# The opening of a diffusion-block kernel: x turned by channel tile, scale and shift by rows, P5 by halves of K in front of P2

## The chip, the cores and the metric

The kernel runs on one core of one Trainium2 chip. The metric is the device time of one execution in microseconds (us), lower is better. Engines: TensorE (PE, matrix products), VectorE (DVE), ScalarE (ACT), GpSimd (POOL) and SyncE (SP), whose queue issues the DMAs. Each works through a list of its own in order; semaphores make one wait for another.

## The reference

One layer of a hybrid diffusion backbone over x (1024 tokens x 1024 channels), all in float32. What the opening of the kernel computes is this part, with `sh1` and `sc1` from a small product of SiLU(c) with `w_mod`:

```
sh1, sc1, gt1, sh2, sc2, gt2 = adaln(c, w_mod, b_mod)
h = rmsnorm(x, g_pre1) * (1 + sc1) + sh1
q, k, v, f, g_a, g_f = split_proj(h @ w_in)
```

Attention over windows, a Fourier branch, the merge of both and a gated convolutional feed-forward net follow. They are not touched by the change.

## The kernel before

**The large products.** `h @ w_in` and `h2 @ w_up` are made by Strassen-Winograd: a pair of 128-wide output columns and two halves of the 1024 tokens give seven products P1 to P7 instead of eight, each over half of K (four tiles of 128 channels). The moving operands come from h: B11, B21, B22 are quarters of it (turned, channels on the partitions, 512 tokens wide), and T1, T2, T3, T4n are their differences. T1 is the token difference of the first four channel tiles; T2 and T4n are taken from T1's raw tile; T3 from the other half. P1 reads B11, P2 B21, P3 B22, P4 T4n, P5 T1, P6 T2, P7 T3. The stationary operands A11 to A22 and their sums S1 to S4 come from the weights. Each product is made of float32 parts: an operand is split into a high part (`hi`, a cast on ACT, L80) and a low part (`lo`, a subtraction on DVE, L68), and three matmuls hi\*hi, hi\*lo, lo\*hi are summed (L85 to L87). An item of four channel tiles is thus 12 matmuls of 128x512.

**The opening** is written out by hand (`with tc.manual_schedule()`): the order of calls is the order of each engine's list. It covers the first 17 items, which are P1, P2, P5, P6 and P7 of the first three pairs (pairs g0, g1, g2), then P4 and P3 of the first. From item 17 on a loop sets the order. The stages:

- Loads. SP issues x (eight tiles of 128 tokens, two halves each), four stages of `w_mod` for shift and scale (`ws`, 256 columns of each a stage, `wm_stage`), the A quarters, the rope tables, and six groups of `w_mod` for the later gates (`wa`, `wm`, `ada_load`). SP keeps eight issues under way and waits for the oldest.
- x. Squares on ACT (`x_square`), root and a Newton step (`x_norm`, two token tiles at a time), scaling by the norm (`x_scale`), turning on PE (`transpose8`, `x_turn`, L162 and L996).
- Shift and scale. `mod_rows` (L581) makes rows of the product with SiLU(c), `mod_copy` (L585) brings them out of PSUM, `mod_turn` (L592) makes columns of them, `mod_vec` adds biases and gains to `ax` and `sx`, two channel tiles a stage, for the latents (c=0) and the context (c=1).
- h. Scale and shift by `affine` (L547 on ACT, L549 on DVE): since a turned token tile has four channel tiles side by side, an instruction covers 128x128. `hraw` holds h by token tile; `hb_puts` and `hb_part` write the operands with one cast and one subtraction per token tile, 384 and 128 wide (or 128 or 256 wide in parts).
- `ada_rows`, `ada_copy` (L749, L753): the gate groups, rows of the product with later columns of `w_mod`.

**Places.** PSUM has eight banks (`ps`, `bufs=8`). The stages `ws`, the gate groups `wa` and the operands other than B11 and T1 share the places of one pool (tag `ha`, ten); a tile that takes over a place is written when the readers of the last one are done.

Of the kernel before, what the change touches and what calls it, by code (L numbers as in the profile page):

```python
# [13 lines left out]
ALU = mybir.AluOpType  # L14
# [26 lines left out]
def block_kernel(ctx: ExitStack, tc: tile.TileContext, t: dict, out: bass.AP, dbg: dict):  # L41
# [497 lines left out]
        else:  # L539
            eng.tensor_scalar(out=xs[tk][h], in0=xs[tk][h], scalar1=xr_[tk], scalar2=1.0, op0=ALU.mult, op1=ALU.mult)  # L540

    def affine(out, src, kh, eng, ks):
        for k in ks:
            a, b = ax[:, 0, kh * 4 + k:kh * 4 + k + 1], sx[:, 0, kh * 4 + k:kh * 4 + k + 1]
            o, i = out[:, k * P:(k + 1) * P], src[:, k * P:(k + 1) * P]
            if eng is None:
                nc.scalar.activation(out=o, in_=i, func=AF.Identity, scale=a, bias=b)  # L547
            else:
                eng.tensor_scalar(out=o, in0=i, scalar1=a, scalar2=b, op0=ALU.mult, op1=ALU.add)  # L549

    def x_turn(tk):
        pt[tk] = transpose8(xs[tk], ps, f"x{tk}")

    pt = {}

    def x_raw(tk):

        hraw[tk, 1] = s(f"hr{tk}1")
        copy(hraw[tk, 1], pt[tk][1])

    def x_first(tk, ks=range(4), kh=0, eng=None):
        if ks[0] == 0:
            hraw[tk, kh] = s(f"hr{tk}{kh}")
        affine(hraw[tk, kh], pt[tk][kh], kh, eng, ks)

    def x_second(tk, ks, eng):
        affine(hraw[tk, 1], hraw[tk, 1], 1, eng, ks)


    modp = {}  # L570
# [24 lines left out]
    def mod_vec(q):  # L595
        k0, ks = 2 * q, slice(2 * q, 2 * q + 2)
        for c in range(2):
            add(sx[:, c, ks], modp[q][:, c:4:2], vec[:, VSH1 + k0:VSH1 + k0 + 2])
            add(ax[:, c, ks], modp[q][:, 4 + c:8:2], vec[:, VSC1 + k0:VSC1 + k0 + 2])
            nc.vector.scalar_tensor_tensor(out=ax[:, c, ks], in0=ax[:, c, ks], scalar=1.0, in1=vec[:, VG1 + k0:VG1 + k0 + 2],  # L600
                                           op0=ALU.add, op1=ALU.mult)


    w_in = t["w_in"]
# [296 lines left out]
    at(NI - 14, lambda: late_loads(0))  # L901
    run, lead, main, pre, conv, sums, mm, evac, after, st = wino(pairs, items, ps, hooks, seng=[nc.vector])
    with tc.manual_schedule():
        for tk in range(4):
            x_load(tk)
        wm_stage(0)
        wm_stage(1)
        for j in range(3):
            pre(j, ("A11",))
        wm_stage(2)  # L910
        wm_stage(3)
        x_load(4)
# [17 lines left out]
        for tk in range(2):  # L930
            for i in range(2):
                x_scale(tk, i, nc.vector)
        x_turn(0)
        x_turn(1)
        x_norm(2)
        mod_rows(0, range(4))
        for tk in range(2, 4):
            for i in range(2):
                x_scale(tk, i, nc.vector)
        x_raw(0)  # L940
        x_raw(1)
        x_turn(2)
        x_turn(3)
        x_raw(2)
        x_raw(3)
        mod_rows(0, range(4, 8))
        mod_copy(0)
        mod_turn(0)
        mod_vec(0)
        def alt_(i):  # L950
            return nc.vector if i % 2 else None

        for c in range(4):
            x_first(c, (0, 1), 0, alt_(c))
        hb_part(hb, "B11", {c: hraw[c, 0] for c in (0, 2, 1, 3)}, 0, 2)
        mod_rows(1, range(8))
        ada_load(0, range(KT))
        conv(0, "P1")
        mm(0, range(2))
        mod_copy(1)  # L960
        conv(1, "P1")
        mod_turn(1)
        mod_vec(1)
        for tk in range(4):
            x_first(tk, (2, 3), 0, alt_(tk))
        mm(1, range(2))
        conv(2, "P1")
        hb_part(hb, "B11", {c: hraw[c, 0] for c in (0, 2, 1, 3)}, 2, 4)
        mm(2, range(2))
        mod_rows(2, range(8))  # L970
        ada_load(1, range(KT))
        mm(0, range(2, 4))
        mod_copy(2)
        mod_turn(2)
        mm(1, range(2, 4))
        mod_vec(2)
        engs = (nc.vector, None, None, nc.vector)
        b21 = {c: hraw[c, 1] for c in (0, 1, 3, 2)}
        for c in range(4):
            x_second(c, (0, 1), engs[c])  # L980
        mod_rows(3, range(4))
        mm(2, range(2, 4))
        mod_rows(3, range(4, 8))
        ada_load(2, range(KT))
        hb_part(hb, "B21", b21, 0, 2)
        conv(0, "P2")
        mod_copy(3)
        mod_turn(3)
        x_square(4)
        x_square(5)  # L990
        mod_vec(3)

        def turn(tk, kh):
            p_ = ps(f"ptx{tk}{kh}")
            for k in range(4):
                nc.tensor.transpose(p_[:, k * P:(k + 1) * P], xs[tk][kh][:, k * P:(k + 1) * P], ident)  # L996
            pt.setdefault(tk, {})[kh] = p_

        def t1(c, eng=None):
            sub(hraw[c, 0], hraw[c + 4, 0], hraw[c, 0], eng)  # L1000

        for c in range(4):
            x_second(c, (2, 3), engs[c])
        hb_part(hb, "B21", b21, 2, 4)
        mm(3)
        x_norm(4)
        for tk in (4, 5):
            x_scale(tk, 0, nc.vector)
        conv(1, "P2")
        x_square(6)  # L1010
        x_square(7)
        for tk in (4, 5):
            turn(tk, 0)
        conv(2, "P2")
        mm(4)
        x_norm(6)
        for tk in (6, 7):
            x_scale(tk, 0, nc.vector)
        for tk in (4, 5):
            x_first(tk, range(4), 0, alt_(tk))  # L1020
        ada_rows(0, 0)
        for tk in (6, 7):
            turn(tk, 0)
        for tk in (6, 7):
            x_first(tk, range(4), 0, alt_(tk))
        mm(5)
        ada_rows(0, 1)
        for c in range(4):
            t1(c)
        sums(0, "S1")  # L1030
        hb_puts(hb, "T1", {c: hraw[c, 0] for c in range(4)})
        conv(0, "P5")
        ada_copy(0)
        ada_load(3, range(KT))
        for tk in range(4, 8):
            x_scale(tk, 1, None)
        ada_rows(1, 0)
        ada_rows(1, 1)
        ada_copy(1)
        ada_load(4, range(KT))  # L1040
        for tk in (4, 5):
            turn(tk, 1)
        for j in range(3):
            evac(j)
        for j in range(3, 6):
            evac(j, True)
        sums(1, "S1")
        conv(1, "P5")
        for tk in (4, 5):
            x_first(tk, range(4), 1)  # L1050
        mm(6)
        for tk in (6, 7):
            turn(tk, 1)
        sums(2, "S1")
        conv(2, "P5")
        for tk in (6, 7):
            x_first(tk, range(4), 1)
        mm(7)
        ada_rows(2, 0)
        for j in range(3):  # L1060
            sums(j, "S3")
            sums(j, "S2")
        conv(0, "P6")
        mm(8)
        ada_rows(2, 1)
        for c in range(4):
            sub(hraw[c, 0], hraw[c + 4, 1], hraw[c, 0])
        hb_puts(hb, "T2", {c: hraw[c, 0] for c in range(4)})
        ada_copy(2)
        ada_load(5, range(KT))  # L1070
        ada_rows(3, 0)
        ada_rows(3, 1)
        conv(1, "P6")
        conv(2, "P6")
        ada_copy(3)
        mm(9)
        ada_rows(4, 0)
        for j in range(4, 9):
            after(j)
        evac(9)  # L1080
        for c in range(4):
            sub(hraw[c + 4, 0], hraw[c + 4, 1], hraw[c + 4, 0])
        mm(10)
        ada_rows(4, 1)
        hb_puts(hb, "T3", {c: hraw[c + 4, 0] for c in range(4)})
        mm(11)
        ada_rows(5, 0)
        for j in range(3):
            conv(j, "P7")
        ada_copy(4)  # L1090
        evac(10)
        evac(11)
        for c in range(4):
            sub(hraw[c, 0], hraw[c, 1], hraw[c, 0])
        for k in range(-12, 12):
            lead(k)
        mm(12)
        ada_rows(5, 1)
        hb_puts(hb, "T4n", {c: hraw[c, 0] for c in range(4)})
        mm(13)  # L1100
        mm(14)
        hb_puts(hb, "B22", {c: hraw[c + 4, 1] for c in range(4)})
        ada_copy(5)
        for k in range(12, 15):
# [1118 lines left out]
```

## Time and profile before

| | us |
|---|---|
| time, median of 3 (1324.95 to 1325.07) | 1325.01 |
| profiled execution, its own time | 1326.39 |
| its span | 1324.6 |
| PE busy | 1266.2 (96%) |
| DVE busy | 1046.2 (79%) |
| ACT busy | 691.2 (52%) |
| first large product starts at | 26.9 |
| first product with T4n starts at | 108.1 |

The page's second part shows the span in 40 slices of 33 us. PE is busy 5 tenths of the first slice and 8 of the next two; from the fourth on it is at 9 almost throughout. DMA is at 9 in the first two. The opening covers the first three slices and a little more. A row of the timeline reads: start, length, engine, line, operation, written tile <- read tiles, shape, number of merged instructions, and in brackets how long the engine was idle before and who ended that. Clock is the share of full speed granted to PE.

### The profile page before, as it was taken

What the parts mean: (1) busy time and instruction counts of PE and PEld (TensorE: products, weight loads), DVE (VectorE), ACT (ScalarE), POOL (GpSimd) and SP (SyncE); (2) the same over time, 40 slices, a digit from 0 to 9 for tenths busy, and PEclk for the clock granted to TensorE, in tenths of its full rate; (3) what the DMA queues carried; (4) which work ended last, traced back from release to release, by engine and by line L of the source; (5) the groups of instructions that cost most, each with busy time, mean ns of one, the idle gap of its engine ahead of it and who ended that gap; (6) DMA issues with size and microseconds to landing.
All of it is one profiled execution on the core that took longest, in us unless ns stands there. A gap on an engine that the chain in (4) does not pass through costs nothing.

```text
span 1324.6 us, 18599 instructions
## 1 busy us (share of the span) xinstructions
PE 1266.2 (96%) x5976; PEld 1021.8 (77%) x5976; DVE 1046.2 (79%) x1954; ACT 691.2 (52%) x1418; POOL 231.3 (17%) x191
## 2 busy tenths in 40 slices
PE   5889999999999999899999999999999999999996
PEld 3457877888878877678877888888888887888884
DVE  4687685976698997676879998999888878666767
ACT  5685245633567775344476655454445445544442
POOL 0000120200243334000000033445545200000000
PEclk9999999999999999999999999999999999999999
DMA  9986275432524443855312487777866668987883
GB/s 307 365 287 204 97 254 175 130 89 85 141 72 121 120 133 99 273 172 162 110 40 67 124 253 233 222 207 222 251 203 198 198 200 292 372 267 223 288 289 144
DMA packets 271575, 254.57 MB, mean 192 GB/s; under 512 B 16733, under 2 KB 206837, under 8 KB 271477
## 3 DMA queue, kind: packets, MB, share of 16 engines
q1 hardware_dynamic: 271476, 253.38, 61.2%
q8 instruction: 47, 0.77, 0.2%
q14 instruction: 52, 0.42, 0.1%
HBM read 179.65 MB, written 73.40 MB: 191 GB/s over the span
## 4 chain that ended last, share of the span: by engine, by line
PE 68%; DVE 15%; DMA 8%; ACT 4%; issue 3%; SPq 2%; POOL 1%; DVEq 0%; ACTq 0%; POOLq 0%
PE X_u L87 5%; PE X_u L85 5%; PE X_u L86 5%; PE X_d L87 3%; PE X_d L85 3%; PE X_d L86 3%; PE Y_u L85 3%; PE Y_u L87 3%; PE Y_u L86 3%; DVE p L1289 2%; PE X_g L85 2%; PE X_g L86 2%; PE X_g L87 2%; DMA ws<-in_w_mod 2%; DVE pl L68 2%
## 5 line engine op out<-in xcount | busy, mean ns | idle before, releaser
L68 DVE TENSOR_TENSOR lP_u<-A_u,hP_u 128x512 fp32r<-128x512 f32 x132 | 106.8, 813 | 22.9 <-ACT hP_u L307 21.3
L369 ACT COPY snP_u<-X_u 128x512 f32<-128x512 f32 x57 | 33.5, 587 | 131.7 <-PE X_u L87 131.6
L369 ACT COPY snP_d<-X_d 128x512 f32<-128x512 f32 x48 | 28.2, 588 | 98.0 <-PE X_d L87 93.8
L307 ACT CAST hP_u<-A_u 128x512 fp32r<-128x512 f32 x121 | 74.7, 620 | 0.0
L1309 POOL TENSOR_SCALAR p<-p,sm 128x640 f32<-128x640 f32 (+1 forms) x64 | 48.5, 780 | 91.7 <-PE pp L1314 35.3
L80 ACT CAST ph<-pp 128x512 fp32r<-128x512 f32 x76 | 44.3, 585 | 22.5 <-PE pp L1314 21.3
L68 DVE TENSOR_TENSOR pl<-pp,ph 128x512 fp32r<-128x512 f32 x76 | 51.6, 681 | 2.5 <-ACT ph L80 2.1
L68 DVE TENSOR_TENSOR yd<-yd,snP_d 128x512 f32<-128x512 f32 x36 | 24.9, 691 | 34.2 <-ACT snP_d L369 34.0
L1303 ACT ACTIVATE p<-p,nm 128x640 f32<-128x640 f32 (+1 forms) x64 | 51.3, 802 | 0.7 <-DVE nm L1296 0.7
L68 POOL TENSOR_TENSOR A_u<-A_u,A_u 128x512 f32<-128x512 f32 x28 | 47.9, 1711 | 13.9 <-DVE lP_u L68 6.1
L1289 DVE CUSTOM_DVE_ANT_0 p<-ss,mask 128x640 f32<-128x640 f32 (+1 forms) x64 | 49.9, 781 | 0.0
L1314 PE MATMUL pp<-ident,p 128*128 128x128 f32 x304 | 46.6, 273 | 2.8 <-POOL p L1309 1.5
L1314 PEld LDWEIGHTS pp<-ident,p 128*128 128x128 f32 x304 | 37.2, 140 | 11.7 <-POOL p L1309 2.9
L1724 DVE SCALAR_TENSOR_TENSOR tb<-u,vec,tb 128x1024 f32<-128x1024 f32 x22 | 39.5, 1797 | 3.1 <-ACT tb L1721 3.1
L68 DVE TENSOR_TENSOR lP_g<-A_g,hP_g 128x512 fp32r<-128x512 f32 x48 | 33.4, 700 | 7.7 <-ACT hP_g L80 7.7
L68 POOL TENSOR_TENSOR S_u<-A_u,A_u 128x512 f32<-128x512 f32 x14 | 23.7, 1696 | 88.3 <-DMA g_d0P<-ghP 81.8
L1285 PE MATMUL ss<-kst,qs 128*128 128x384 f32 (+1 forms) x128 | 36.6, 368 | 1.3 <-DVE mx L1289 0.8
L1725 DVE SCALAR_TENSOR_TENSOR tb<-u,vec,tb 128x1024 f32<-128x1024 f32 x22 | 36.5, 1658 | 0.9
L68 POOL TENSOR_TENSOR A_u<-S_u,A_u 128x512 f32<-128x512 f32 x14 | 18.7, 1338 | 104.1 <-DVE lP_u L68 101.7
L68 DVE TENSOR_TENSOR wB<-wB,wB 128x512 f32<-128x512 f32 x44 | 36.0, 817 | 0.0
L1325 PE MATMUL po<-pl,vst 128*128 128x512 f32 x76 | 31.3, 411 | 2.8 <-DVE pl L68 2.3
L1728 ACT ACTIVATE tb<-tb 128x1024 f32<-128x1024 f32 x22 | 23.4, 1063 | 16.6 <-DVE tb L1725 16.6
(887 smaller groups left out, 4378.7 us busy)
## 6 DMA issues: line engine op xcount, KB each, us to landing
A_u<-in_w_up SPq DMA_DIRECT2D x88, 256.0 KB, 4.6
wB<-in_w_down SPq DMA_DIRECT2D x44, 256.0 KB, 4.4
wa<-in_w_mod SPq DMA_DIRECT2D x36, 256.0 KB, 5.3
wt_dT<-wB SPq DMA_DIRECT2D x33, 256.0 KB, 2.3
wdB<-in_w_down SPq DMA_DIRECT2D x33, 256.0 KB, 4.4
wdT<-wt_dT SPq DMA_DIRECT2D x33, 256.0 KB, 3.2
A_g<-in_w_in SPq DMA_DIRECT2D x32, 256.0 KB, 5.5
ws<-in_w_mod SPq DMA_DIRECT2D x30, 256.0 KB, 6.0
```

The costliest lines, as they stand in the source:

```text
L68: return (eng or nc.vector).tensor_tensor(out=out, in0=a, in1=b, op=op)
L80: copy(hi, src)
L85: nc.tensor.matmul(ps, ah, bh, start=start, stop=False, skip_group_check=True)
L86: nc.tensor.matmul(ps, ah, bl, start=False, stop=False, skip_group_check=True)
L87: nc.tensor.matmul(ps, al, bh, start=False, stop=stop, skip_group_check=True)
L307: copy(st[j]["half", p][0], st[j][STA[p]])
L369: copy(d["s" + p], d["X"])
L1289: nc.vector.tensor_tensor_reduce(out=p_, in0=ssc[:, lo:768], in1=self.mk, op0=ALU.add, op1=ALU.max, scale=1.0, scalar=-3.0e38, accum_out=s ...
L1303: nc.scalar.activation(out=self.pt[g], in_=self.pt[g], func=AF.Exp, scale=SCALE, bias=self.m[:, g:g + 1], accum_out=self.sm[:, g:g + 1])
L1309: nc.gpsimd.tensor_scalar(out=self.pt[g], in0=self.pt[g], scalar1=self.sm[:, g:g + 1], scalar2=1.0, op0=ALU.mult, op1=ALU.mult)
L1314: nc.tensor.transpose(pp[:, g * P:(g + 1) * P], self.pt[g][:, j * P:(j + 1) * P], ident)
L1724: nc.vector.scalar_tensor_tensor(out=tb, in0=u[:, 0:1024], scalar=cw[0], in1=tb, op0=ALU.mult, op1=ALU.add)
```

## The change

Nothing is computed otherwise. In the opening:

- Turning goes by channel tile: `x_turn(half, k)` puts one channel tile of four token tiles into one bank, so that scale and shift are one column pair for a whole 128x512 bank. `x_mod` does them in one instruction; `x_raw`, `x_first`, `x_second` and `affine` go. `hraw` is kept by channel tile, and `x_put` splits one of them into its part of an operand: one cast and one subtraction of 128x512.
- `mod_vec` is called for latents and context apart, the latents first.
- Token tiles 4 to 7 of x are requested ahead of the third `w_mod` stage; the A quarters are spread among the stages; the rope tables come behind three gate groups.
- P5 of the first two pairs is made by halves of K ahead of P2; P5 of the third comes behind P2.
- T1, T2, T3 and T4n are made a channel tile at a time: subtraction, cast, low part.
- The gate groups are read later, each whole, behind P5 and between the items of P6, P7 and P4.
- `warm(n)` turns the identity into a bank that nothing reads, 6, 8 and 8 times, at three places where PE waits.

On DVE, the operand T3 (`hr` is `hraw`). Before:

```order
L68 TENSOR_TENSOR hr_695<-hr_842,hr_695 128x512
L68 TENSOR_TENSOR hr_700<-hr_847,hr_700 128x512
L68 TENSOR_TENSOR hr_720<-hr_881,hr_720 128x512
L68 TENSOR_TENSOR hr_725<-hr_886,hr_725 128x512
L68 TENSOR_TENSOR T3a_249<-hr_695,T3a_248 128x3x128
L68 TENSOR_TENSOR T3a_249<-hr_700,T3a_248 128x3x128
L68 TENSOR_TENSOR T3a_249<-hr_720,T3a_248 128x3x128
L68 TENSOR_TENSOR T3a_249<-hr_725,T3a_248 128x3x128
```

and now:

```order
L68 TENSOR_TENSOR hr_556<-hr_735,hr_556 128x512
L68 TENSOR_TENSOR T3a_245<-hr_556,T3a_244 128x512
L68 TENSOR_TENSOR hr_558<-hr_737,hr_558 128x512
L68 TENSOR_TENSOR T3a_245<-hr_558,T3a_244 128x512
L68 TENSOR_TENSOR hr_596<-hr_774,hr_596 128x512
L68 TENSOR_TENSOR T3a_245<-hr_596,T3a_244 128x512
L68 TENSOR_TENSOR hr_598<-hr_776,hr_598 128x512
L68 TENSOR_TENSOR T3b_247<-hr_598,T3b_246 128x512
```

Four subtractions stood ahead of the low parts; now each low part, which reads what its cast on ACT wrote (T3a_244), stands between two subtractions.

On ACT, the casts of T4n and what stands around them, with the semaphores that each waits for. Before:

```order
L297 COPY snP_g_1086<-X_g_476 128x512 [waits DVE_49,PE_49]
L80 CAST T4na_252<-hr_372 128x3x128 [waits DMAHW4_49,DMAHW5_49,DMAHW3_49,DVE_49]
L80 CAST T4na_252<-hr_375 128x3x128 [waits DVE_49]
L80 CAST T4na_252<-hr_378 128x3x128 [waits DVE_49]
L80 CAST T4na_252<-hr_381 128x3x128 [waits DVE_49]
```

and now:

```order
L755 COPY ac_1005<-ar_996 128x512 [waits PE_49,Activation_49]
L80 CAST T4na_248<-hr_356 128x512 [waits DMAHW4_49,DMAHW3_49,DMAHW5_49,DVE_49,PE_49]
L80 CAST T4na_248<-hr_358 128x512 [waits DVE_49]
L80 CAST T4na_248<-hr_427 128x512 [waits DVE_49]
L80 CAST T4nb_250<-hr_429 128x512 [waits DVE_49]
L755 COPY ac_1040<-ar_1031 128x512 [waits DMAHW5_49,PE_49]
```

The first cast stood behind copies of products; now it stands between the copies of two gate groups, and waits for PE.

On PE, what stands ahead of the first product with T4n. Before:

```order
L85 MATMUL X_g_476<-T3b_250,hP_g_1078 128x512
L86 MATMUL X_g_476<-T3b_251,hP_g_1078 128x512
L87 MATMUL X_g_476<-T3b_250,lP_g_1079 128x512
L85 MATMUL X_g_417<-T4na_252,hP_g_1174 128x512
L86 MATMUL X_g_417<-T4na_253,hP_g_1174 128x512
```

and now:

```order
L85 MATMUL X_g_412<-T3b_246,hP_g_968 128x512
L86 MATMUL X_g_412<-T3b_247,hP_g_968 128x512
L87 MATMUL X_g_412<-T3b_246,lP_g_969 128x512
L751 MATMUL ar_1091<-wa_936,sv_119 32x512 x3
L751 MATMUL ar_1091<-wa_940,sv_119 32x512 x3
L751 MATMUL ar_1091<-wm_6_944,sv_119 32x512
L751 MATMUL ar_1091<-wm_7_946,sv_119 32x512
L85 MATMUL X_g_367<-T4na_248,hP_g_1062 128x512
```

The sixth gate group was read among the items of P7; now it stands whole between the last of P7 and the first of P4.

The diff, cut to its core (helpers, loads, and the calls that the prediction speaks of):

```diff
-    def x_turn(tk):
-        pt[tk] = transpose8(xs[tk], ps, f"x{tk}")
+    def x_turn(half, k, cs=range(4)):
+        if cs[0] == 0:
+            pt[half, k] = ps(f"x{half}{k}")
+        for c in cs:
+            nc.tensor.transpose(pt[half, k][:, c * P:(c + 1) * P], xs[half * 4 + c][k // 4][:, k % 4 * P:(k % 4 + 1) * P], ident)
...
+    def x_mod(half, k, eng=None):
+        o, a, b = s(f"hr{half}{k}"), ax[:, 0, k:k + 1], sx[:, 0, k:k + 1]
+        if eng is None:
+            nc.scalar.activation(out=o, in_=pt[half, k], func=AF.Identity, scale=a, bias=b)
+        else:
+            eng.tensor_scalar(out=o, in0=pt[half, k], scalar1=a, scalar2=b, op0=ALU.mult, op1=ALU.add)
+        hraw[half, k] = o
+
+    def x_put(o, k, src):
+        split(mov[o][0][k], mov[o][1][k], src)
...
+    def warm(n):
+        if not idle:
+            idle.append(ps("idle"))
+        for i in range(n):
+            nc.tensor.transpose(idle[0][:, :P], ident, ident)
...
+        pre(0, ("A11",))
         wm_stage(0)
+        pre(1, ("A11",))
+        pre(2, ("A11",))
         wm_stage(1)
+        for tk in range(4, 8):
+            x_load(tk)
+        wm_stage(2)
+        for j in range(2):
+            pre(j, ("A21", "A22"))
+        wm_stage(3)
...
+        mod_copy(0)
+        warm(6)
+        mod_turn(0)
+        mod_vec(0, 0)
+        warm(8)
+        for k in range(2):
+            x_mod(0, k, V if k else None)
...
+        def t1(k):
+            sub(hraw[0, k], hraw[1, k], hraw[0, k])
+            x_put("T1", k, hraw[0, k])
...
+        for k in range(2):
+            t1(k)
+        conv(0, "P5")
...
+        mm(6, range(2))
...
+        for k in range(2):
+            t2(k)
+        for k in range(6, 8):
+            x_mod(1, k)
...
+        mm(5)
...
+        mm(10)
+        evac(9)
         ada_rows(2, 0)
+        for k in range(4):
+            sub(hraw[1, k], hraw[1, k + 4], hraw[1, k])
+            x_put("T3", k, hraw[1, k])
...
         mm(12)
+        ada_rows(3, 0)
+        ada_rows(3, 1)
+        ada_copy(3)
+        for k in range(4):
+            sub(hraw[0, k], hraw[0, k + 4], hraw[0, k])
+            x_put("T4n", k, hraw[0, k])
         mm(13)
+        ada_rows(4, 0)
+        ada_rows(4, 1)
+        ada_copy(4)
         mm(14)
+        for k in range(4):
+            x_put("B22", k, hraw[1, k + 4])
```

More of the change, by code (lines that the diff above doesn't have):

```diff
@@ L929, in block_kernel @@
             x_square(tk)
[L930 to L934, printed above, removed]
+        for i in range(2):
+            for tk in range(2):
+                x_scale(tk, i, V)
+        for k in range(4):
+            x_turn(0, k, range(2))
         x_norm(2)
@@ L950, in alt_ @@
[L950 to L955, printed above, removed]
+        mod_vec(0, 0)
+        warm(8)
+        for k in range(2):
+            x_mod(0, k, V if k else None)
+        mod_vec(0, 1)
+        for k in range(2):
+            x_put("B11", k, hraw[0, k])
+        mm(0, range(2))
+        conv(1, "P1")
+        mm(1, range(2))
+        conv(2, "P1")
@@ new lines, in block_kernel @@
+        x_turn(0, 4)
+        x_turn(0, 5)
+        mod_vec(1, 1)
+        for k in range(2, 4):
+            x_put("B11", k, hraw[0, k])
+        warm(8)
+        mm(0, range(2, 4))
+        x_square(4)
+        x_square(5)
+        mm(1, range(2, 4))
+        x_norm(4)
+        for tk in (4, 5):
+            x_scale(tk, 0, V)
+        mm(2, range(2, 4))
+        mod_rows(2, range(4))
+        x_square(6)
+        x_square(7)
+        x_norm(6)
+        for tk in (6, 7):
+            x_scale(tk, 0, V)
@@ L983, in block_kernel @@
+        x_turn(0, 6)
+        x_turn(0, 7)
+        mm(7, range(2))
+        for k in range(2):
+            x_put("B21", k, hraw[0, k + 4])
         mod_rows(3, range(4, 8))
         ada_load(2, range(KT))
-        hb_part(hb, "B21", b21, 0, 2)
-        conv(0, "P2")
[L987 to L1008, printed above, removed]
+        rope_load()
+        mod_copy(3)
+        mm(6, range(2, 4))
+        mod_turn(3)
+        mod_vec(3, 0)
+        for k in range(2, 4):
+            x_mod(0, k + 4, V if k % 2 else None)
+        mm(7, range(2, 4))
@@ L1009, in block_kernel @@
+        conv(0, "P2")
+        mod_vec(3, 1)
+        for k in range(2, 4):
+            x_put("B21", k, hraw[0, k + 4])
+        mm(3, range(2))
         conv(1, "P2")
[L1010 to L1013, printed above, removed]
+        for tk in range(4, 8):
+            x_scale(tk, 1, None)
+        mm(3, range(2, 4))
         conv(2, "P2")
-        mm(4)
[L1016 to L1020, printed above, removed]
@@ L1021, in block_kernel @@
-        ada_rows(0, 0)
[L1022 to L1026, printed above, removed]
-        ada_rows(0, 1)
[L1028 to L1032, printed above, removed]
+        for k in range(4, 6):
+            x_turn(1, k)
+        sums(2, "S1")
+        for k in range(4, 6):
+            x_mod(1, k)
+        evac(3, True)
@@ new lines, in block_kernel, with t2 @@
+        mm(4)
+        for k in range(6, 8):
+            x_turn(1, k)
+        def t2(k):
+            sub(hraw[0, k], hraw[1, k + 4], hraw[0, k])
+            x_put("T2", k, hraw[0, k])
+        conv(2, "P5")
+        for k in range(2):
+            t2(k)
+        for k in range(6, 8):
+            x_mod(1, k)
+        evac(4, True)
+        sums(0, "S3")
+        sums(0, "S2")
+        mm(5)
+        for k in range(2, 4):
+            t2(k)
+        conv(0, "P6")
+        evac(5, True)
+        mm(8)
```

165 lines of the change are left out of this document (50 added, 115 removed).

## The prediction

> **What bounds the kernel now.** I read three views: busy time by stretches, the opening on TensorE (PE) in order of time, and what PE waits for later. The stretches first; columns are stretch, its length, PE busy (instructions), granted clock, DMA share, GB/s.
>
> ```profile
> 0.00:27.00 27.00, 12.27 (x75) 1.00 0.96 298
> 27.00:108.00 81.00, 71.71 (x364) 0.94 0.93 313
> 108.00:200.00 92.00, 92.00 (x419) 1.00 0.58 187
> ```
>
> PE lacks 14.7 us up to 27 us and 9.3 us more up to 108 us, and from there to 200 us it never idles. What it waits for from 108 us to the end (the three longest; us in total, times, longest):
>
> ```profile
> PE Y_d L85 <- DVE yd L68: 2.4, 2, 1.3
> PE po L1325 <- DVE pl L68: 2.3, 7, 0.5
> PE pa L85 <- ACT whpa L1573: 2.1, 1, 2.1
> ```
>
> No row of that list names a load, and all its waits are on work behind PE itself. So a delay at 108 us reaches the end one for one. The opening on PE, from start to the landmark I use, the first product that reads T4n:
>
> ```profile
> 12.50 3.68 PE L162 MATMUL ptx<-ident,x 128*128 128x128 f32 x16 [8.33 <-DVE x L540]
> 26.90 0.50 PE L85 MATMUL X_g<-B11a,hP_g 128*128 128x512 f32 x1 [1.92 <-ACT hP_g L80]
> 43.65 0.40 PE L87 MATMUL X_g<-B11b,lP_g 128*128 128x512 f32 x1
> 50.57 0.50 PE L85 MATMUL Z_g<-B21a,hP_g 128*128 128x512 f32 x1 [2.08 <-ACT B21a L80]
> 67.45 0.66 PE L996 MATMUL ptx<-ident,x 128*128 128x128 f32 x4 [1.11 <-ACT x L538]
> 69.76 1.11 PE L996 MATMUL ptx<-ident,x 128*128 128x128 f32 x4 [1.65 <-ACT ac L753]
> 87.01 0.50 PE L86 MATMUL X_g<-T2a,hP_g 128*128 128x512 f32 x1 [0.82 <-DVE T2a L68]
> 108.14 0.39 PE L85 MATMUL X_g<-T4na,hP_g 128*128 128x512 f32 x1
> ```
>
> The waits are short and ended by DVE or ACT: the opening is bound by hand-overs between the three engines, each of which works its own list in order. The change keeps what is computed and rewrites those lists, so I lay the new lists out with the durations below and see when the landmark comes.
>
> **The durations.** DVE and ACT:
>
> ```profile
> 82.59 2.49 DVE L68 TENSOR_TENSOR hr<-hr,hr 128x512 f32<-128x512 f32 x4
> 87.68 0.69 DVE L68 TENSOR_TENSOR lP_g<-A_g,hP_g 128x512 fp32r<-128x512 f32 x1
> 73.47 0.69 DVE L68 TENSOR_TENSOR lP_g<-S_g,hP_g 128x512 fp32r<-128x512 f32 x1 [0.76 <-ACT hP_g L80]
> 37.73 0.69 DVE L585 COPY mc<-mr 128x512 f32<-128x512 f32 x1 [2.51 <-PE mr L581]
> 43.75 0.62 ACT L507 ACTIVATE junk<-x 128x512 f32<-128x512 f32 x1
> 44.50 0.63 ACT L507 ACTIVATE junk<-x 128x512 f32<-128x512 f32 x1
> 56.62 1.49 ACT L547 ACTIVATE hr<-ptx,sx,ax 128x128 f32<-128x128 f32 x4
> 66.68 2.56 ACT L538 ACTIVATE x<-x,rx 128x512 f32<-128x512 f32 x4
> 72.82 0.62 ACT L80 CAST hP_g<-S_g 128x512 fp32r<-128x512 f32 x1 [1.66 <-DVE S_g L68]
> 83.31 2.32 ACT L80 CAST T2a<-hr 128x384 fp32r<-128x384 f32 x4 [3.24 <-DVE hr L68]
> 88.45 1.28 ACT L657 ACT_TABLE_LOAD   x1
> 89.75 1.67 ACT L657 ACTIVATE c_g<-c_g 128x512 f32<-128x512 f32 x3
> ```
>
> and PE, with two rows of the slow clock:
>
> ```profile
> 53.23 1.06 PE L996 MATMUL ptx<-ident,x 128*128 128x128 f32 x8 [0.87 <-DVE x L540]
> 89.73 1.07 PE L749 MATMUL ar<-wa,sv 128*32 128x512 f32 x8
> 32.09 0.63 PE L86 MATMUL X_g<-B11a,hP_g 128*128 128x512 f32 x1
> 32.51 0.63 PE L87 MATMUL X_g<-B11a,lP_g 128*128 128x512 f32 x1
> 30.00:40.00 10.00, 10.00 (x45) 6.45 (x46) 4.97 (x21) 3.60 (x13) 0.00 (x0) 0.73 1.08 360
> ```
>
> An item of twelve products takes 2.7 us (the rows 0.23 apart at full clock), a turn 0.13, eight row products of a group 2.0. A DVE operation on 128x512 occupies 0.60, a cast on ACT 0.52.
>
> **The price of one row of a difference.** The operands T1, T2, T3 and T4n are subtraction, high part (ACT), low part (DVE). Before, four subtractions ran first and the casts ran beside them and the lows: 82.59 to 87.68, 5.1 us of DVE. Now the list reads subtraction, low, subtraction, low, and each low waits for its own cast. From a subtraction's start to its cast's start are 0.72 us (82.59 to 83.31), from a cast to its low 0.65 (72.82 to 73.47), and the low occupies 0.60: 1.97 a row, 7.9 an operand. The cheapest bound, the cast wholly hidden, is 1.2 a row; I take 1.97, since the list leaves DVE nothing to do between.
>
> **Step 1, up to the first product: gains.** Turns from 12.5 us, now 8, then four row products, 8 turns, four row products at the same pace as before (the row at 12.50 is slow clock: 0.23 each): 19.3. Copy, 0.8: 20.1. Four small products and three small vector operations, 1.6. Scale and shift of 128x512 on ACT is not in the trace: between 0.52 (a cast) and 1.5 (four 128-wide ones, 56.62); I take 0.68, a cast plus what the scale column adds to a narrow one. Cast 0.65. First product at 23.3, against 26.90. The 14 unread turns lie in these waits.
>
> **Step 2, P1: gains.** Halves for two pairs with 0.5 of waiting for lows, a row group (2.0), the third half: 29.9. Small products 1.0, two turned column tiles 1.0 with 0.9 of waiting for a bank that a scaling on ACT frees; eight unread turns 1.0, beside the low of the last row; three second halves: 38.0. Row group 2: 40.0. Before, P1 ended at 44.1 (row 43.65), five microseconds of its products at half clock (row 32.09), with row group 2 and half of group 3 done: 2 to 4 us ahead by equal work.
>
> **Step 3, x of the second half: -2.1.** ACT reaches the eight squares (0.75 apart, rows 43.75 and 44.50) only behind the B11 casts, at 33.4; they end at 39.6 with the first root among them, the second norm's eight small operations and two scalings on DVE at 42.4. x is requested 12 us sooner, but no engine reads it sooner than that. PE waits 2.1; turns, small products and half a row group are done at 46.4.
>
> **Step 4, T1: -4.0.** The vectors are there at 44.7; two scalings and a sum on DVE end at 46.6; row 0 takes 1.97; row 1 its subtraction and cast, 1.24; then the cast of the pair's own S1 on ACT, 0.65, which stands behind both: first product of P5 at 50.5. The rest of P5, B21 and P2 loses some 4.7 in waits of 0.3 to 1.4 (lows of rows 2 and 3, the row copy behind two lows, four scalings of x of 0.64 on ACT): 71.6 with the turns done.
>
> **Step 5, the third item of P2: -4.3.** It needs the bank of a turned tile, freed by a scaling on ACT, which stands behind the casts of T2's rows 0 and 1, so behind two subtractions on DVE. P2's second item ends at 70.3; copying out and the cast of S1 0.9, its low 0.6, row 0 1.97, row 1's subtraction and cast 1.24, the scaling 0.8: 75.9.
>
> **Step 6, T3: -4.7.** P2, P5, a gate group, P6, a gate group, P6: 90.8 is the start of gate group 2. T3's tiles lie where that group's weights lay (its cast waits for PE), so the first cast can start at 92.4; a table load, three sigmoids and a copy on ACT (3.5 us behind gate group 1) end at the same time. Row 3's cast ends 3 x 1.97 + 0.62 later, then a row copy and the cast of the pair's S3: first P7 product at 100.2. PE has 4.7 us of work between.
>
> **Step 7, T4n: -5.0.** P7, gate group 3, P7: 107.9 is the start of gate group 4, whose place T4n takes. First cast 1.2 later, row 3's cast ends 6.6 after it (the first low adds a little), then a row copy, four B22 casts and the pair's own A22, six ACT operations, 3.2, with 0.6 of latencies: 119.6. PE has 6.7 us of work between.
>
> **The sum.** The old lists laid out with the same durations put the landmark at 107.7, 0.4 ahead of its row, so I compare with that: 119.6 is 11.9 us late. Loads do not decide: three are put ahead of the second row stage, whose last issue stands below; three more at some 0.75 and a landing of 6.0 give 26.0, and that group is read from 26.6. x and row stage 2 land by 32 and 38, read at 33.4 and 38.0; the latter is tight, and up to two microseconds late there are swallowed by step 3.
>
> ```profile
> 17.72 0.37 SPq L484 DMA_DIRECT2D wm<-in_w_mod  x1
> ws<-in_w_mod SPq DMA_DIRECT2D x30, 256.0 KB, 6.0
> ```
>
> **The clock.** Gaps of 4 us and more now stand ahead of P2's third item, P7 and P4, and PE is the bound right behind each. In the trace the clock is at half behind 2.8 us of idling in some four (rows 67.45 and 69.76):
>
> ```profile
> 70.97 0.79 PE L85 MATMUL Y_g<-T1a,hP_g 128*128 128x512 f32 x1
> 72.84 0.47 PE L86 MATMUL Y_g<-T1a,hP_g 128*128 128x512 f32 x1
> ```
>
> Four products take 1.87 there for 0.91, 1.0 lost. At 30 to 35 us twelve products 0.42 apart lose 2.3. Three drops cost 3.0 to 6.9, and nothing if none comes (the gap of 2.08 at 50.57 brought none). I take three at 0.9, a little under the one that follows a gap: 2.7. The Trainium skill, page "TensorE: Matmul & The Clock Gate", section "What's actually happening", has the clock halved after an idle window of about 3.4 us and restored after a busy one. By that rule, estimated, each of the three gaps costs 1.7, 5.1 in all; the trace halves the clock without such a gap, so it is stricter than the rule.
>
> The profiled execution took 1326.39 us with 1.8 around its span of 1324.6; the median is 1325.01, 1.4 less. I add the difference to the median: 1325.0 + 11.9 + 2.7 = 1339.6.
>
> **Rivals.** *No drop of the clock*: 1336.9; for it, the gap at 50.57. *Dear drops*, three at 2.3: 1343.8; for it, the clock of 0.73 in the row of 30 to 40. *Half-hidden rows*, 1.2 instead of 1.97: T1 and the third P2 item gain 1.5 each, T3 and T4n 2.3 each, 7.6 in all, 4.3 late: 1329.3; against it the list. *Faster, the loads pace the opening*: the chain of waits runs over gate loads up to 71 us.
>
> ```profile
> 66.17 5.28 DMA wa<-in_w_mod
> 71.44 0.67 DVE c_g L68
> ```
>
> If that is the bound, gate groups that are read later free the opening: step 1 gives 3.6, the clock 3.3, and half of the 9.3 us that PE lacks between 27 and 108 go: 1325 - 11.5 = 1313.5. It decides where PE's waits end with the landing of a gate group. Against it: those waits name ACT and DVE. *The lead of step 2 just pays the stalls*: same. *The unread turns do not hold the clock*: then P1 loses up to 2.3, which the wait of step 3 swallows; the forecast stands.
>
> **How the numbers follow.** Forecast 0.40, no drop 0.25, dear drops 0.15, half-hidden 0.08, same 0.04, faster 0.08. About 0.2% is what a measurement of this kernel can tell from no change. Slower 0.88, same 0.04, faster 0.08. The range runs from the half-hidden case to just over the dear drops, 1329 to 1345.
>
> **What would show it.** Right: the first product near 23.3; a PE wait of some 4 us ended by ACT ahead of P5's first item, of P2's third, of the first P7 and the first P4; DVE rows of T3 about 2 us apart; the first T4n product at 120 to 126. Wrong: those four waits under 2 us, or lows of T1 to T4n back to back; then the landmark comes before 114. Steps 1 and 2 are wrong if P1 ends behind 41.

## The result, and the profile after

The change made the kernel slower: 1343.84 us (median of 4, 1342.66 to 1344.93) against 1325.04 for the kernel before on the same chip; the ratio is 1.0141, 95% interval 1.0123 to 1.0158. The forecast was 1339.6, range 1329 to 1345. The profiled execution after took 1343.85, its span 1342.1.

Busy time of the profile after in the stretches that were shown of before (columns: stretch, length, PE, PEld, DVE, ACT, POOL busy with instructions, granted clock, DMA share, GB/s):

```profile
0.00:27.00 27.00, 14.06 (x63) 8.20 (x64) 12.17 (x41) 14.11 (x31) 0.31 (x5) 0.96 0.95 298
27.00:108.00 81.00, 65.98 (x322) 43.43 (x322) 48.14 (x101) 39.98 (x75) 0.00 (x0) 0.86 0.74 250
108.00:200.00 92.00, 87.72 (x409) 65.95 (x408) 59.27 (x96) 37.05 (x68) 15.37 (x10) 0.97 0.58 185
```

PE did 1.8 us more up to 27 us, 5.7 us less from there to 108, at a clock of 0.86 instead of 0.94, and it still idles 4.3 us behind 108, where it had not idled before. The opening on PE after:

```profile
23.78 0.50 PE L85 MATMUL X_g<-B11a,hP_g 128*128 128x512 f32 x1 [1.10 <-ACT B11a L80]
44.23 1.32 PE L547 MATMUL x<-ident,x 128*128 128x128 f32 x6 [1.86 <-DVE x L540]
53.52 0.79 PE L85 MATMUL Y_g<-T1a,hP_g 128*128 128x512 f32 x1 [2.75 <-ACT hP_g L80]
78.75 0.50 PE L85 MATMUL Z_g<-B21a,hP_g 128*128 128x512 f32 x1 [4.13 <-ACT hr L555]
104.73 0.80 PE L85 MATMUL X_g<-T3a,hP_g 128*128 128x512 f32 x1 [4.09 <-ACT hP_g L80]
126.45 0.50 PE L85 MATMUL X_g<-T4na,hP_g 128*128 128x512 f32 x1 [4.28 <-ACT snP_g L297]
```

The first product comes 3.1 us sooner than before (26.90). Then four waits stand ahead of P5, P2's third item, P7 and P4, each ended by ACT, and the landmark, the first product that reads T4n, is 18.3 us late (108.14 before). That is the loss: behind it the remaining execution is as long as before (1343.85 - 126.45 = 1217.4; 1326.39 - 108.14 = 1218.3). The list of PE's waits from 108 us on has one new entry at its top, the wait ahead of P4; the next is as before:

```profile
PE X_g L85 <- ACT snP_g L297: 4.6, 2, 4.3
PE Y_d L85 <- DVE yd L68: 2.4, 2, 1.3
```

What DVE does in T3, and the first cast of T4n on ACT, which waits for PE's reads of the gate group whose place it takes:

```profile
97.77 0.69 DVE L68 TENSOR_TENSOR T3a<-hr,T3a 128x512 fp32r<-128x512 f32 x1 [5.35 <-ACT T3a L80]
99.75 0.69 DVE L68 TENSOR_TENSOR T3a<-hr,T3a 128x512 fp32r<-128x512 f32 x1 [0.69 <-ACT T3a L80]
101.73 0.69 DVE L68 TENSOR_TENSOR T3a<-hr,T3a 128x512 fp32r<-128x512 f32 x1 [0.68 <-ACT T3a L80]
```
```profile
116.06 0.62 ACT L80 CAST T4na<-hr 128x512 fp32r<-128x512 f32 x1 [3.26 <-PE ar L751]
```

Lows of one operand start 1.98 us apart. And the clock, in three stretches of the profile after:

```profile
24.50:28.00 3.50, 3.49 (x8) 2.74 (x9) 1.76 (x3) 0.79 (x2) 0.00 (x0) 0.52 1.06 393
44.20:58.40 14.20, 11.35 (x46) 8.13 (x47) 9.73 (x21) 5.78 (x9) 0.00 (x0) 0.53 1.10 357
101.00:110.00 9.00, 5.27 (x12) 3.80 (x12) 4.53 (x8) 4.25 (x8) 0.00 (x0) 0.62 0.12 47
```

### The profile page after: what moved, and what is told of

The parts are those of the page before. It is cut to its first block, busy times and chain, and to the rows that moved or that the text cites. A ratio compares the mean times of both kernels' runs of the same rounds, so it can differ in the third digit from the quotient of the medians.

```text
span 1342.1 us, 18506 instructions
## 1 busy us (share of the span) xinstructions
PE 1277.3 (95%) x5998; PEld 1029.8 (77%) x5998; DVE 1041.7 (78%) x1899; ACT 679.0 (51%) x1349; POOL 231.5 (17%) x191
## 4 chain that ended last, share of the span: by engine, by line
PE 69%; DVE 15%; ACT 6%; DMA 4%; issue 3%; SPq 1%; POOL 1%; DVEq 0%; ACTq 0%; POOLq 0%
PE X_u L87 5%; PE X_u L85 5%; PE X_u L86 5%; PE Y_u L85 3%; PE X_d L86 3%; PE X_d L87 3%; PE X_d L85 3%; PE Y_u L86 3%; PE Y_u L87 3%; PE X_g L85 2%; DVE p L1308 2%; PE X_g L86 2%; PE X_g L87 2%; DVE pl L68 2%; PE Y_d L85 1%
```

## The experiments

The theory: the order of the lists on DVE and ACT makes the four waits (1.97 us a row of a difference, a bank freed late, two operands that wait for a gate group's place), and half clock behind the waits adds to them. The rivals: the places alone, the clock alone, the loads. Unless a diff says otherwise, the base is the changed kernel. All ratios are to the kernel before, run beside it; its medians lay between 1325.0 and 1326.8.

| run | median us | ratio (95%) | profiled execution us | landmark us |
|---|---|---|---|---|
| the change | 1343.84 | 1.0141 (1.0123 to 1.0158) | 1343.85 | 126.45 |
| again | 1343.39 | 1.0137 (1.0120 to 1.0154) | 1342.50 | 123.72 |
| rows | 1331.07 | 1.0034 (1.0024 to 1.0045) | 1329.04 | 111.28 |
| places | 1340.91 | 1.0109 (1.0095 to 1.0123) | 1341.05 | 122.19 |
| fill | 1340.54 | 1.0105 (1.0091 to 1.0119) | 1341.49 | 124.06 |
| nowarm | 1345.99 | 1.0148 (1.0134 to 1.0162) | 1345.64 | 126.02 |
| xlate | 1349.77 | 1.0176 (1.0163 to 1.0189) | 1349.45 | 131.31 |
| whole | 1347.00 | 1.0160 (1.0145 to 1.0175) | 1348.29 | 130.48 |
| p5late | 1352.36 | 1.0198 (1.0179 to 1.0218) | 1354.17 | 135.33 |
| rows + squares (sq6) | 1326.52 | 1.0002 (0.9993 to 1.0012) | 1327.38 | 110.88 |
| rows + bank (t2early) | 1327.15 | 1.0008 (1.0000 to 1.0017) | 1326.30 | 110.70 |
| relist | 1317.81 | 0.9938 (0.9926 to 0.9950) | 1317.72 | 101.23 |

### The rows of the differences: subtractions together

```diff
         for k in range(4):
             sub(hraw[1, k], hraw[1, k + 4], hraw[1, k])
+        for k in range(4):
             x_put("T3", k, hraw[1, k])
```

The same in T4n, and by pairs of rows in T1 and T2.

> The change with one thing different: in T1 and T2 the two subtractions of a pair of rows stand together ahead of their casts and lows, in T3 and T4n all four do. Theory A (a row of a difference costs 1.97 us because subtraction and low alternate): the lows of T3 come 0.6 us apart, the wait ahead of the first P7 product goes from 4.1 us to under 0.5, those ahead of P5's first item and P2's third fall by about 1.4 each, the one ahead of P4 from 4.3 to about 2.4; the first product that reads T4n comes at 111 to 115 instead of 126.5, with fewer half-clock stretches, and the time is 1328 to 1332 us. Theory B (the places of the gate groups' weights hold T3 and T4n, whatever the order on VectorE): the waits ahead of P7 and P4 stay above 2.5 us and the time is 1336 to 1340. Theory C (the loss lies in the clock, not in the waits): the waits shrink, the half-clock stretches stay, 1338 to 1342.

In the profile of this run T3's lows are one row again on DVE, its casts one row on ACT (starts, then the time of three):

```profile
91.56 1.90 DVE L68 TENSOR_TENSOR T3a<-hr,T3a 128x512 fp32r<-128x512 f32 x3 [3.55 <-ACT T3a L80]
```
```profile
90.68 1.66 ACT L80 CAST T3a<-hr 128x512 fp32r<-128x512 f32 x3
```

and on PE the wait ahead of P7 is gone; what is left is

```profile
49.86 0.80 PE L85 MATMUL Y_g<-T1a,hP_g 128*128 128x512 f32 x1 [2.62 <-ACT hP_g L80]
72.57 0.50 PE L85 MATMUL Z_g<-B21a,hP_g 128*128 128x512 f32 x1 [2.76 <-ACT hr L555]
111.28 0.50 PE L85 MATMUL X_g<-T4na,hP_g 128*128 128x512 f32 x1 [2.47 <-ACT snP_g L297]
```

Theory A holds in its rows, its landmark (111.28) and its time, at its upper half. Of the 18 us, 12.5 (by the medians) to 14 (by the ratios) hang on the order of subtractions and lows, and with the waits went part of the half clock behind them: the four waits together are 9.2 us shorter than in the second execution of the change (the run named again), the landmark 12.4 sooner. Places alone and clock alone fall.

### The places: gate groups read earlier

```diff
+        ada_rows(2, 0)
+        ada_rows(2, 1)
         mm(10)
...
         ada_rows(3, 1)
+        ada_rows(4, 0)
+        ada_rows(4, 1)
         ada_copy(3)
```

(and taken out where they stood).

> The change with gate group 2 read ahead of the second P6 item instead of behind the third... that is one item of twelve products earlier, and gate group 4 right behind group 3; the rows of the differences stay subtraction, low, subtraction, low. Theory A (rows at 1.97 us decide, the place only where the cast has nothing else to wait for): the wait ahead of P7 stays at 4 us or more, because the sigmoids and the table load on ScalarE end at about the time the place comes free; the wait ahead of P4 falls from 4.3 to about 2, since T4n's first cast starts some 2.5 us sooner: 1340 to 1342.5 us against 1343.8 for the change. Theory B (the places decide): both waits fall by 2.5 or more, the half clock behind them goes too, 1334 to 1338.

```profile
103.38 0.80 PE L85 MATMUL X_g<-T3a,hP_g 128*128 128x512 f32 x1 [4.31 <-ACT hP_g L80]
122.19 0.79 PE L85 MATMUL X_g<-T4na,hP_g 128*128 128x512 f32 x1 [2.40 <-ACT snP_g L297]
```

The wait ahead of P7 is 4.31 (4.09 without the edit), the one ahead of P4 fell to 2.40: theory A in both. At T3 the sigmoids hold the first cast just as long as the place does; at T4n the place is the last thing waited for.

### The clock: the gaps filled with work that nothing reads

```diff
+        hold(28)
         mm(12)
...
+        hold_wide(5)
         for k in range(15, 17):
```

`hold(n)` makes n turns of the identity, 128 wide, into a bank of its own; `hold_wide(n)` n products of 128x512.

> The change with 28 unread 128-wide turns ahead of the first P7 item (3.6 us of the 4.1 us wait there) and 5 unread 512-wide f32 products ahead of the first P4 item (some 2.3 us of the 4.3). Nothing that is read changes. In the change the clock is at half for 4.9 us behind the first gap and some 3 us behind the second. Theory A (a busy TensorE holds the clock, whatever the width): both half-clock stretches go, 4.0 us less, 1339 to 1341. Theory B (turns of 128 columns do not count as work, products of 512 do): the stretch behind P7 stays at 12 products 0.42 us apart, the one behind P4 goes, 1341.5 to 1343. Theory C (neither counts): 1343 to 1345.

PE at the first gap and the clock behind it (the wide products then stand from 120.06 to 124.1, and P4 runs at full clock too):

```profile
99.28 3.22 PE L927 MATMUL hold<-ident 128*128 128x128 f32 x28
103.52 0.50 PE L85 MATMUL X_g<-T3a,hP_g 128*128 128x512 f32 x1 [1.03 <-ACT hP_g L80]
120.06 4.56 PE L932 MATMUL hold<-rope,sel 128*128 128x512 f32 x10 [1.19 <-ACT ac L755]
```
```profile
103.50:106.50 3.00, 2.98 (x12) 2.10 (x12) 2.50 (x4) 1.98 (x4) 0.00 (x0) 1.00 0.00 0
```

Both drops are gone, behind narrow turns as behind wide products: theory A, 3 us less by the medians, 4 to 5 by the ratios. This is one profile; in the seven others in which the wait ahead of P7 stands unfilled at 4.1 to 4.3 us, the item behind it ran at half clock. The five products took 4.6 us, twice what I had allowed, so P4 started about 1.3 us later than it could: from the first P7 product to the first P4 product are 20.5 us, where the change less its drop (21.7 - 2.5) has 19.2.

### The 22 unread turns taken away

```diff
-        warm(6)
...
-        warm(8)
```

> The change without the 22 unread turns. Theory A (they do not hold the clock: the half clock from 24.5 to 28.0 us came in spite of them): the same half-clock stretch in P1, and 1342 to 1346 us. Rival (they shorten the drop): without them the first half of P1 runs at half clock from its first product, 2 us and more are lost ahead of the second half of x and nothing swallows them, 1346 to 1348.

```profile
24.50:28.00 3.50, 3.50 (x10) 2.53 (x9) 1.13 (x2) 0.17 (x1) 0.00 (x0) 0.57 1.06 394
```

Theory A: the same half clock in P1, and a ratio whose interval overlaps that of the change. By the ratios the turns bought 1 to 1.5 us, which the intervals do not tell from nothing; the medians are 2.2 and 2.6 apart, but those of the kernel before, run beside them, differ by 1.5 to 1.7. In the run named fill, where turns did hold the clock, they stood where PE idled for 4 us. The waits that the change put them into are 0.9, 2.0 and 1.1 us long without them.

### The change once more

> The change once more, unaltered, beside the other two. Theory A (the half clock in the first half of P1 comes in some executions and not in others, since the lists up to there are the same in runs that had it and runs that had not): 1342 to 1345 us, the clock between 24 and 28 us may be 0.5 or 1.0, the four waits of 2.7 to 4.3 us behind it stand as they were. Rival (the half clock there belongs to the change): it is there again, from 24.5 to 28 us.

The profile of this run has the clock at 1.00 where the first one had 0.52, with the same lists:

```profile
24.50:28.00 3.50, 3.50 (x19) 2.22 (x23) 1.70 (x3) 0.74 (x2) 0.00 (x0) 1.00 1.06 392
```

and the opening on PE reads

```profile
23.73 0.49 PE L85 MATMUL X_g<-B11a,hP_g 128*128 128x512 f32 x1 [1.10 <-ACT B11a L80]
42.62 1.17 PE L547 MATMUL x<-ident,x 128*128 128x128 f32 x6 [1.86 <-DVE x L540]
51.09 0.79 PE L85 MATMUL Y_g<-T1a,hP_g 128*128 128x512 f32 x1 [4.00 <-ACT hP_g L80]
76.18 0.74 PE L85 MATMUL Z_g<-B21a,hP_g 128*128 128x512 f32 x1 [4.13 <-ACT hr L555]
102.14 0.80 PE L85 MATMUL X_g<-T3a,hP_g 128*128 128x512 f32 x1 [4.09 <-ACT hP_g L80]
123.72 0.53 PE L85 MATMUL X_g<-T4na,hP_g 128*128 128x512 f32 x1 [4.79 <-ACT snP_g L297]
```

Theory A: the half clock in P1 belongs to the execution, not to the change. The landmark comes 2.7 us sooner without it. Of these, 1.6 are there when the turns go on (42.62 and 44.23); most of the rest arises between there and P5, where the first execution ran at half clock (0.53 from 44.2 us) and this one at full clock up to its wait of 4.00. At the end 1.4 are left (1342.50 and 1343.85).

### x of the second half requested late again

```diff
-        for tk in range(4, 8):
-            x_load(tk)
         wm_stage(2)
-        for j in range(2):
-            pre(j, ("A21", "A22"))
         wm_stage(3)
+        for tk in range(4, 8):
+            x_load(tk)
+        for j in range(2):
+            pre(j, ("A21", "A22"))
```

> The change with one part undone: x of the second half is requested behind the fourth row stage again, where it was before; the lists of the engines are those of the change. Theory A (the earlier request is worth what lies between its landing and the place where ScalarE can read it): x lands some 3 to 4 us after ScalarE is free for the squares, and the norms of its second two tiles come later still; the wait ahead of the turns of the second half, 1.9 us in the change, becomes 6 to 8 us in one or two pieces, the rest follows unchanged: 1348 to 1351 us. Rival (squares stand behind the B11 casts anyway, so the request is worth nothing): 1343 to 1345.

The first square of x's second half now waits for the load, and the wait ahead of the turns came in two pieces, 5.9 us for 1.9:

```profile
38.94 0.63 ACT L507 ACTIVATE junk<-x 128x512 f32<-128x512 f32 x1 [4.40 <-DMA x<-in_x]
```

```profile
44.21 0.78 PE L547 MATMUL x<-ident,x 128*128 128x128 f32 x2 [3.30 <-DVE x L540]
47.63 1.73 PE L547 MATMUL x<-ident,x 128*128 128x128 f32 x6 [2.64 <-DVE x L540]
```

Theory A, with a wait just under its 6 to 8 us. With the new lists the earlier request is worth 5 us by the ratios, 6 by the medians (1349.8 against 1343.6, the mean of the change's two).

### Six squares earlier on ACT, with the rows together

```diff
         mod_turn(1)
+        for tk in range(4, 7):
+            x_square(tk)
         mod_vec(1, 0)
```

(the seventh and eighth behind the B11 casts; base: rows).

> The order with the subtractions together (the run rows), and six of the eight squares of x's second half ahead of the second pair of scalings on ScalarE, where that engine idles 8 us, instead of behind the B11 casts; the last two stay behind them. Theory A (step 3's wait is the squares' place on ScalarE, not the landing of x): the wait of 1.9 us ahead of the turns goes to under 0.5 and the first product that reads T4n comes about 2 us sooner than in rows: 1328.5 to 1329.5 where rows has 1331. Rival (the wait only moves to P5's first item, which is bound by the chain of T1): that wait grows by as much, and the time is that of rows.

The wait ahead of the turns is gone. The one ahead of P5 is 2.62 as in rows, so it did not take it over; between the two stands one of 0.43, which rows has too:

```profile
45.69 1.07 PE L575 MATMUL mr<-ws,sv 128*32 128x512 f32 x8 [0.43 <-DVE hr L557]
```

Theory A in the waits; the time, 1326.5, is under its range. The medians are 4.5 us apart, against 2 expected, the profiled executions 1.7; this profile had the half clock in P1 and that of rows had not, so the landmarks (110.88 and 111.28) do not show the gain whole. Its size stays between 1.7 and 4.5.

### The bank of P2's third item freed earlier, with the rows together

```diff
+        for k in range(6, 8):
+            x_mod(1, k)
         conv(2, "P5")
         t2(0)
-        for k in range(6, 8):
-            x_mod(1, k)
         evac(4, True)
```

(base: rows)

> The order of the run rows, and the scaling of the last two column tiles, which frees the bank of P2's third item, ahead of T2's casts on ScalarE instead of behind the first two. Theory A: the wait of 2.8 us ahead of P2's third item goes to under 0.5, but T2's third and fourth rows then are late for P6, whose first product gets a wait of 1 to 1.5 us that rows does not have; 0.8 us or a little more are left, 1329.5 to 1330.5 where rows has 1331. Rival: the whole 2.8 us and the half clock behind the wait are gained, 1327 to 1328.5.

The wait of 2.76 is gone, and the one forecast ahead of P6 is there:

```profile
80.79 0.50 PE L85 MATMUL X_g<-T2a,hP_g 128*128 128x512 f32 x1 [1.30 <-ACT hP_g L80]
```

So theory A's mechanism, but the time came out better than it said, 3.9 us under rows by the medians (2.7 by the profiled executions), in the rival's range: with the wait the half clock behind it went too (0.60 in rows from 72.5 to 76, shown at the end).

### P5's items whole, and P5 behind P2's first item

Whole:

```diff
-        mm(6, range(2))
...
-        mm(7, range(2))
...
-        mm(6, range(2, 4))
+        mm(6)
...
-        mm(7, range(2, 4))
+        mm(7)
```

Behind P2's first item, instead:

```diff
         mm(3, range(2, 4))
+        mm(6)
+        mm(7)
         conv(2, "P2")
```

> The change with P5's first two items whole, each where its second half of K stood; the lists of ScalarE and VectorE are those of the change. Theory A (the row that comes last decides, a half that runs early only moves idle time): P5's first product comes some 3 us later than in the change and a wait of about 4 us stands in front of the turns there, but P5's last product, which waits for T1's last low and for the turned vectors, comes at the same time: 1342 to 1345 us, as the change. Rival (the halves are worth the products that they put into the wait, two of 1.4 us): 1345.5 to 1347.

> The change with P5's first two items whole and behind P2's first item, where P2 waits for the scalings of B21: P5 in front of P2 undone on TensorE, the other lists as in the change. Theory A (P5 fills the wait for B21, its two items of 2.7 us are work that stands in a gap): a wait of 6 us or more ahead of the turned vectors of the fourth stage, P2 starts at the same time and everything behind it is 4 to 5 us later: 1347 to 1350. Rival (the two items are hidden later, in the wait for P2's third item, which ScalarE and VectorE set): 1343 to 1345.

With whole items the last hand-over came when it did with halves: from the second half of x (44.79 in that profile, 44.23 in the change) to the fourth stage's small products are 17.8 and 18.1 us. But the second item's twelve products, all behind it now, met the half clock:

```profile
62.50:70.00 7.50, 7.39 (x22) 6.10 (x23) 4.04 (x12) 5.23 (x10) 0.00 (x0) 0.54 0.97 367
```

They took 5.3 us (64.07 to 69.34) for 2.7. So the halves are worth some 3 us (3.4 by the medians, 1347.0 against 1343.6), which is the rival's range; not by the products they put into the wait, as it says, but, as this one profile has it, because fewer products are left behind the last wait when the clock is low. With P5 behind P2's first item, the gap that P5 had filled is open:

```profile
61.77 1.84 PE L586 MATMUL pm<-sel,mc 128*128 128x2 f32 x8 [5.43 <-DVE mc L579]
65.50 0.80 PE L85 MATMUL Z_g<-B21a,hP_g 128*128 128x512 f32 x1 [1.89 <-ACT hP_g L80]
```

1352.4, 8 to 9 us more than the change where theory A said 4 to 5; of its sign and place there is no doubt, the rest is probably clock again (0.50 from 58.4 to 70 us in that profile, 0.99 in the change). Of the parts undone here, P5 in front of P2 is worth most.

### All lists rewritten

Rows together, six squares early, the bank's scaling ahead of T2, gate groups 2 and 4 read earlier, and more moves, of which these are the core (base: the change):

```diff
         for k in range(2):
             x_mod(1, k)
+        sums(0, "S1")
+        t1(0)
+        conv(0, "P5")
+        for k in range(2, 4):
+            x_turn(1, k)
         mod_vec(2, 0)
...
+        mm(6, range(2))
+        conv(1, "P5")
         mod_rows(3, range(4))
...
+        lead(12)
+        evac(12)
         for k in range(4):
             x_put("B22", k, hraw[1, k + 4])
```

(and the row copy of the fourth stage ahead of B21's casts). The edit also rewrites PE's list, which the expectation does not name: the first half of P5 stands ahead of the fourth stage's row products, and two column tiles are turned behind T1's first rows.

> All of it in one: the subtractions together, six squares early, the bank's scaling ahead of T2, gate groups 2 and 4 read earlier, T1's first two rows ahead of the scalings of B21 and of the vectors on VectorE, the row copy of group 3 ahead of B21's casts, and the cast of the first P4 item ahead of B22's casts. Theory A (the opening is bound by the order of the lists on ScalarE and VectorE, and what is ahead at 108 us reaches the end one for one): the first product that reads T4n comes at 100 to 103 us, against 108.1 before the change, no wait on TensorE between 27 and 108 us is over 2 us, and the time is 1317 to 1321, faster than both. Rival (loads or the clock then pace the opening, or later work takes the lead back): the landmark comes early but the time is 1323 to 1327.

Its opening, by stretches and in two rows of PE:

```profile
27.00:108.00 81.00, 75.54 (x423) 48.70 (x423) 59.75 (x121) 51.14 (x97) 0.00 (x0) 1.00 0.95 313
```
```profile
44.87 0.50 PE L85 MATMUL Y_g<-T1a,hP_g 128*128 128x512 f32 x1 [1.86 <-ACT hr L555]
101.23 0.50 PE L85 MATMUL X_g<-T4na,hP_g 128*128 128x512 f32 x1
```

From the first product to the landmark the longest wait is that of 1.86; the clock is 1.00; the landmark is 6.9 us ahead of before and the time 8.5 us (ratio 0.9938, 0.9926 to 0.9950). Theory A; this version beats both kernels. What each move is worth in it is not told. The loads set no bound here: they moved 313 GB/s from 27 to 108 us, as before the change, and PE's longest waits there name ACT.

## Why the prediction was right, and where it was off

The sign, the mechanism and the range were right; the time was 4.2 us short (1339.6 for 1343.8), and of its cases the dear drops, 1343.8 at 0.15, came out, not the forecast. That this case agrees to the tenth is luck: it puts 6.9 us on three drops, which measured 6.0, and nothing on two stretches of half clock that came besides (P1, and from the turns to P5). By its steps, with the execution that had no half clock in P1 beside the first one:

| step | predicted us | again | the change |
|---|---|---|---|
| 1, first product | 23.3 | 23.73 | 23.78 |
| 2, row group 2 starts | 38.0 | 38.46 | 40.08 |
| 3, turns of the second half go on | 42.1 | 42.62 | 44.23 |
| 4, first P5 product | 50.5 | 51.09 | 53.52 |
| 5, P2's third item | 75.9 | 76.18 | 78.75 |
| 6, first P7 product | 100.2 | 102.14 | 104.73 |
| 7, first T4n product, no drops | 119.6 | 123.72 | 126.45 |

**Steps 1 to 5** hold within 0.6 us in the execution without the drop in P1, and their waits too (step 4: 4.0 and 4.00; step 5: 4.3 and 4.13). In the first execution the wait of step 4 is 2.75, since the turns and row products ahead of it ran at half clock and took up part of it. Scaling 128x512 on ACT, for which I took 0.68 between bounds of 0.52 and 1.5, took 0.78 alone and 1.45 for two; that is small beside the rest.

**Steps 6 and 7** are off by the clock. In the second execution P2's third item behind step 5's wait took 4.45 us (76.18 to 80.63) for 2.73, the P7 item behind step 6's 5.1 for 2.7: 4.1 us together, and 119.6 + 4.1 is its 123.7. The four waits are the predicted ones and the rows 1.98 us apart; the run rows shows the price by undoing it.

**The term that was mis-sized is the clock's.** I took three drops at 0.9, 2.7 us, from the four products behind the gap in the trace of before; in the first execution they measured 1.7 (78.75 to 83.20), 2.5 (104.73 to 110.0) and 1.8 (P4's first item, 126.45 to 130.99), 6.0 together against 2.73 an item, inside the bounds of 3.0 to 6.9. (Behind its filled wait in fill the P7 item took 3.2, 103.52 to 106.74; against that the 2.5 would be 2.1.) Four products were the end of a drop that had begun earlier; the item at half clock, from which I had the 2.3, was the nearer row. The Trainium skill, page "TensorE: Matmul & The Clock Gate", section "What's actually happening", has a full window of about 3.4 us at half clock; the estimate from it, 1.7 each and 5.1 in all, was nearer to the 6.0 than my choice. Those 3.3 us are most of the 4.2, but the rest does not come out clean. Half clock in P1 and from the turns to P5 had put the first execution 2.6 us behind the second by step 5 (78.75 and 76.18), which is more than is left; and behind the landmark its execution took 0.9 us less than that of before, although P4's first item lost 1.8 there. So one for one, as the prediction has it for a delay at 108 us, holds within 2 us or so; what made up for the loss behind the landmark was not traced.

**The unread turns.** The prediction priced their failure at nothing, because the wait of step 3 would swallow what P1 loses. That sentence is wrong. In the execution with the drop the wait of step 3 is 1.86, in the one without it 1.86 as well, and the turns resume 1.6 us later. What ends the wait, the squares, stands on ACT behind the B11 casts, and these behind the second row stage on PE, which stands behind the half of P1 that was slow: the squares began at 35.52 in the one execution and 33.91 in the other. A wait swallows a delay only when what ends it does not hang on what was delayed.

**The rivals.** That loads pace the opening fell: no wait of the four names a DMA, and relist, 8.5 us shorter, moved the same 313 GB/s. Half-hidden rows fell on the rows. "Same" fell: P1 ends 4 us sooner (5.5 in the second execution) and that does not pay the stalls. By equal work step 2's lead was smaller than its 2 to 4 us: when P1 ended, the kernel before had also made a third round of small products (39.01) and eight more turns, about 1 us each, which the prediction does not count. With them and the half row group the change is about 1 us ahead in the second execution and not ahead in the first.

## What to carry to other kernels

Before a list is rewritten, ask of each instruction on an in-order engine what it waits for and what independent work stands behind it: subtraction, low, subtraction, low against subtractions first, by fours or pairs, was 12.5 to 14 of 18 us, with the same instructions and the half clock behind the waits counted in. Price a gap on TensorE together with the item behind it, which can run at half clock throughout; to find out whether it does, fill the gap with work that nothing reads. And a gain early in the list (3 us to the first product here) is worth only as much as the later hand-overs let through, so lay the list out to a landmark behind which nothing waits.

## What the hardware showed that was not expected

The length of a gap alone did not decide the clock behind it. All 21 waits of 4.09 to 4.80 us that stood unfilled ahead of P2's third item, P7 and P4 were followed by half clock. Shorter ones differed. Of the waits ahead of P4, 2.40 in the run places was followed by half clock, 2.47 in rows, sq6 and t2early by full clock; these are the second products behind them, in places and in rows:

```profile
122.78 0.63 PE L86 MATMUL X_g<-T4na,hP_g 128*128 128x512 f32 x1
```
```profile
111.62 0.40 PE L86 MATMUL X_g<-T4na,hP_g 128*128 128x512 f32 x1
```

The wait of 1.85 to 1.88 ahead of the turns was followed by half clock in seven profiles, the change's first among them, and by full clock in again and rows. In relist, whose longest wait from the first product to the landmark is 1.86, the clock stayed at 1.00. Within rows itself, 2.62 and 2.76 were followed by half clock and 2.47 by full clock (72.5 to 76 behind 2.76, 111.2 to 114 behind 2.47):

```profile
72.50:76.00 3.50, 3.43 (x9) 2.74 (x10) 3.38 (x7) 1.56 (x4) 0.00 (x0) 0.60 0.00 0
111.20:114.00 2.80, 2.65 (x10) 1.91 (x11) 2.80 (x6) 2.37 (x6) 0.00 (x0) 1.00 1.06 394
```

So the clock fell here behind gaps shorter than the 3.4 us of idling that the Trainium skill states on the page named above, and not behind all of them. In P1, behind the same wait of 1.1 us and the same list up to there, it fell in seven profiles and not in four. The same page says that the window runs on by itself, so that the point of change depends on where in it the work falls; executions that differ fit that, but what makes the window count as idle there stays open, and no run here tells it.
